# The address distance between the two operands of every fp32r matmul

## The chip, the cores and the metric

The kernel runs on one core of a Trainium2 chip. The metric is the device time of one execution in microseconds (us), of which the median over several executions is given. A profiled execution has, beside its time, a span (from the first to the last instruction) and a trace of every instruction.

A word that is used throughout: a *step* is the time from the start of one matmul to the start of the next one on TensorE.

## The reference, cut to what matters

The kernel computes a two-layer transformer encoder on one sequence of 512 tokens with 1024 channels, in float32. The sizes set the number of matmuls:

```python
def window_gqa_sink(h, w_qkv, w_out, sink):         # layer 0: 16 query heads, 4 key/value heads
    qkv = h @ w_qkv                                 # 1024 -> 1536
    ...
    o, lse = banded_attention(q, k, v, slopes, 1, WINDOW_A, BLOCK_A)
    o = o * jax.nn.sigmoid(lse - sink...)[..., None]
    return o... @ w_out                             # 1024 -> 1024

def dilated_mixture_attention(h, w_qkv, w_out):     # layer 1: three groups of 16 heads
    qkv = (h @ w_qkv).reshape(b, s, N_GROUPS_B, 3, H_B, HEAD_DIM)    # 1024 -> 9216
    ...
    return o... @ w_out

def swiglu(h, w_gate, w_up, w_down):                # after each attention
    return (jax.nn.silu(h @ w_gate) * (h @ w_up)) @ w_down           # 1024 -> 2816 -> 1024

def reference(x, ...):
    for i in range(DEPTH):                          # 2
        x = x + attention_i(rmsnorm(x, norm_mix[i]))
        x = x + swiglu(rmsnorm(x, norm_ffn[i]), w_gate[i], w_up[i], w_down[i])
    return rmsnorm(x, norm_final)
```

## The kernel before

Everything is kept transposed: channels on the 128 partitions, the 512 tokens along the free axis. Each float32 operand is split into a high and a low part of type fp32r (`split`, line 91: ScalarE rounds to the high part, VectorE subtracts to get the low part), and each product is the sum of three fp32r products: high by high, high by low, low by high. This is `mm3` (line 113). It issues its matmuls with 256 moving columns each; with a result of 512 columns that makes six matmuls for one block of 128 by 128 weights.

A matmul has two operands. The *stationary* one (128 columns, 512 bytes in each partition) is put into the array by a weight load; the *moving* one (256 columns, 1024 bytes in each partition) then streams through it. Every matmul of this kernel has a weight load of its own, even where two in a row use the same block.

Three kinds of product go through `mm3`:

- `unit` (line 170), and the output and down projections: the stationary operand is a weight block (`wh` or `wl`), the moving one the activations: `xh`, `xl` (normalised input), `oh`, `ol` (attention output) or `ah`, `al` (the hidden layer of the SwiGLU). In the rows of the profile these are `mm<-xh,wh`, `tp<-xh,wh`, `sc<-ah,wh` and so on: result, moving operand, stationary operand.
- `values` (line 189): here the activations are stationary and the weights move: `psv<-wh,xh`.
- The attention scores in fp32r do not use `mm3` but have the same form: `score_pair` (line 137) in layer 0, with queries `qt` stationary and keys `kt`, `kl` moving, in pieces of 256 or 384 columns; and `scores_a` (line 620) for the first head group of layer 1, with `qs` stationary and `ks`, `kl` moving.

The order of the work on TensorE is written out by hand: generators yield after each block of weights, and `weave` and `spread` place a given number of such pieces between the attention's steps. The SwiGLUs (`swiglu`, line 494) have no such weaving; they are two runs of over 3,000 `mm3` matmuls with nothing between.

Memory is handed out by pools, in the order in which tiles are first asked for, each size rounded up to 32 bytes. Pools stand behind each other: `const` (`x`, `xh`, `xl` and small tables), `wpool` (three buffers of 4096 bytes each for raw weights, `wh` and `wl`), `spool` (small temporaries), and then one pool for the stage that runs: `l0`, `ffn` or `l1`. All operands of the fp32r products are tiles of 2048 bytes in a partition or multiples of it, and they are read in pieces that begin at multiples of 512 bytes from the tile's start. So the distance between the two operands of such a matmul, taken modulo 512, is the same for all matmuls on the same pair of tiles, whichever buffer and whichever block it is. The addresses that the build gives are, as bytes modulo 512:

| tiles | before | with the change |
|---|---|---|
| `wh`, `wl` | 0 | 0 |
| `xh`, `xl` | 192 | 256 |
| `ah`, `al`, `oh`, `ol` | 192 | 256 |
| layer 0: `kt`, `kl` / `qt` | 192 / 192 | 256 / 0 |
| layer 1: `ks`, `kl` / `qs` | 192 / 192 | 0 / 256 |

From this follows the distance, moving minus stationary, modulo 512:

| products | before | with the change |
|---|---|---|
| weights stationary (`unit`, projections), 9,888 matmuls | 192 | 256 |
| activations stationary (`values`), 1,248 matmuls | 320 | 256 |
| fp32r scores, 256 matmuls | 0 | 256 |

Of the kernel before, what the change touches and what calls it, by code (L numbers as in the profile page):

```python
# [9 lines left out]
F32 = mybir.dt.float32  # L10
# [8 lines left out]
H = 16  # L19
# [45 lines left out]
def trunk(ctx, tc, xT, gains, sink, tabs, qsc, wunits, wv, outT):  # L65
# [4 lines left out]
    const = ctx.enter_context(tc.tile_pool(name="const", bufs=1))  # L70
    wpool = ctx.enter_context(tc.tile_pool(name="wpool", bufs=3))
    spool = ctx.enter_context(tc.tile_pool(name="spool", bufs=2))
    psum = ctx.enter_context(tc.tile_pool(name="psum", bufs=2, space=bass.MemoryType.PSUM))
    BUFS = {"mm": 3, "sc": 2, "tp": 2, "ov": 1}

# [2 lines left out]

    x = const.tile([128, NK, S], F32, name="x")
    qs_sb = const.tile([128, 16], F32, name="qs_sb")  # L80
    xh = const.tile([128, NK, S], F32R, name="xh")
    xl = const.tile([128, NK, S], F32R, name="xl")
    g_sb = const.tile([128, 5, NK], F32, name="g_sb")
    sink_sb = const.tile([128, H], F32, name="sink_sb")
    nsink = const.tile([128, H], F32, name="nsink")
    tab = const.tile([128, 1024], F32, name="tab")
    ident = const.tile([128, 128], F32, name="ident")
# [37 lines left out]
    def split_queries(q, pair):  # L125
        for a, (own, other) in enumerate((HALVES, HALVES[::-1])):
            nc.scalar.activation(pair[a][own], q[own], AF.Copy)
            nc.vector.tensor_tensor(pair[a][other], q[own], pair[a][own].bitcast(F32), op=OP.subtract)  # L128

    def split_keys(k, pair, low):  # L130
        for a, (own, other) in enumerate((HALVES, HALVES[::-1])):
            nc.scalar.activation(pair[a][own], k[own], AF.Copy)
            nc.scalar.activation(pair[a][other], pair[a][own].bitcast(F32), AF.Copy)
            nc.vector.tensor_tensor(low[a][own], k[own], pair[a][own].bitcast(F32), op=OP.subtract)
            nc.scalar.activation(low[a][other], low[a][own].bitcast(F32), AF.Copy)
# [34 lines left out]
    def unit(u, hi, lo, tag, done, cuts=(0, NK)):  # L170


        def gen():
            tiles = weight_tiles()
            wh, wl = chunks(tiles, (NK, 128))
            ps = bank(tag)
            for j in range(NK):
                if j in cuts:
                    load(tiles, wunits[u], slice(128 * j, 128 * cuts[cuts.index(j) + 1]))
                mm3(ps, wh[:, j], wl[:, j], hi[:, j, :], lo[:, j, :], j == 0, j == NK - 1)  # L180
                if j == NK - 1:
                    if norm["wait"] is None:
                        done(ps)
                    else:
                        norm["wait"].append(lambda: done(ps))
                yield
        return NK, gen()
# [110 lines left out]
    with tc.tile_pool(name="l0", bufs=2) as pool:  # L298
# [14 lines left out]
        def q_unit(P, i, **kw):  # L313
            def done(ps):
                t = spool.tile([128, S], F32, name="tmp")
                col = 4 * P + i
                nc.vector.scalar_tensor_tensor(t, ps, qs_sb[:, col:col + 1], norm["rb"], op0=OP.mult, op1=OP.mult)
                qk["q", P, i] = [pool.tile([128, S], F32R, name=f"qt{a}", bufs=8) for a in range(2)]
                split_queries(t, qk["q", P, i])
            return unit(5 * P + 1 + i, xh, xl, "mm", done, **kw)  # L320
# [239 lines left out]
    with tc.tile_pool(name="l1", bufs=2) as pool:  # L560
# [9 lines left out]
        def qk_units(p, g):  # L570

            def views(out, *src):
                if g:
                    return (out, *src)
                return (out.rearrange(IN_ORDER, m=16), *[t.rearrange(BY_CLASS, m=16) for t in src])

            def q_done(ps):
                name = "q1" if g else "qa"
                qk["q", p, g] = q = pool.tile([128, S], F32, name=name, bufs=2 if g else 1)
                out, src, rb = views(q, ps, norm["rb"])  # L580

                for to, at in ((slice(4, 32), slice(0, 28)), (slice(0, 4), slice(28, 32))) if g == 0 else [(slice(None),) * 2]:
                    nc.vector.scalar_tensor_tensor(out[..., to], src[..., at], qs_sb[:, 8 + p:9 + p], rb[..., at],
                                                   op0=OP.mult, op1=OP.mult)
                if g == 0:
                    qk["qs", p] = [pool.tile([128, S], F32R, name=f"qs{a}", bufs=1) for a in range(2)]
                    split_queries(q, qk["qs", p])

            def k_done(ps):
                name = "k1" if g else "ka"  # L590
                qk["k", p, g] = k = pool.tile([128, S], F32, name=name, bufs=2 if g else 1)
                out, src, rb = views(k, ps, norm["rb"])
                nc.vector.tensor_tensor(out, src, rb, op=OP.mult)
                if g == 0:
                    qk["ks", p] = [pool.tile([128, S], F32R, name=f"ks{a}", bufs=1) for a in range(2)]
                    qk["kl", p] = [pool.tile([128, S], F32R, name=f"kl{a}", bufs=1) for a in range(2)]
                    split_keys(k, qk["ks", p], qk["kl", p])

            at = u1 + 6 * p + 2 * g
            return [unit(at, xh, xl, "mm", q_done), unit(at + 1, xh, xl, "mm", k_done)]  # L600

        def v_unit(pg, g):
# [356 lines left out]
```

## Time and profile before

| | |
|---|---|
| median of three executions | 1472.33 us (1470.74 to 1473.45) |
| the profiled execution | 1473.99 us |
| its span | 1472.3 us |
| granted TensorE clock, mean | 0.996 |
| TensorE busy | 1453.9 us (99%), 12,820 matmuls |
| VectorE / ScalarE / GpSimd busy | 732.6 / 613.9 / 109.1 us |
| DMA | 128.29 MB, 87 GB/s |
| the two SwiGLUs, from their first matmul on | about 193 to 553 us and 1104 to 1457 us of the span |

The profiled execution is 1.66 us above the median. TensorE is busy all through, so what matters is the step and not the waits. A matmul's own duration in the trace (276 to 287 ns in the large groups) is more than two steps long, because matmuls are pipelined; the rate must be read from the starts or from the length of a piece of the chain of waits divided by its count.

### The profile page before, as it was taken

How to read it: one execution, taken by the hardware profiler on the slowest of the kernel's cores; microseconds unless marked ns; L12 is line 12 of the kernel's file. 1: busy time of each engine (PE TensorE's matmuls, PEld its weight loads, DVE VectorE, ACT ScalarE, POOL GpSimd, SP SyncE). 2: the span in 40 equal slices, each digit the busy share in tenths (PEclk: the TensorE clock that was granted, in tenths of full speed). 3: DMA queues.
4: the chain of work that ended last, by engine and by line, in shares of the span. 5: the costliest groups of instructions: out<-in, count | busy, mean ns of one | idle time of the engine just before them, and what ended most of it. 6: DMA issues, size and time to landing. Idle time of an engine off the chain costs nothing.

```text
span 1472.3 us, 29609 instructions
## 1 busy us (share of the span) xinstructions
PE 1453.9 (99%) x12820; PEld 1426.7 (97%) x12820; DVE 732.6 (50%) x1400; ACT 613.9 (42%) x1126; POOL 109.1 (7%) x152
## 2 busy tenths in 40 slices
PE   8999999999999999999999999999999999999997
PEld 8988999999999999999999999999999999999997
DVE  6776544444443345346556556556464444443223
ACT  6776433322323335445545536536343322332221
POOL 3334200000000010000000000000030000000111
PEclk9999999999999999999999999999999999999998
DMA  6110232323223232312212122222132322232331
GB/s 201 58 59 15 87 101 87 101 101 100 94 87 104 94 111 69 101 63 86 79 67 87 58 87 73 72 87 73 44 116 86 101 101 98 90 101 91 96 103 57
DMA packets 38450, 128.29 MB, mean 87 GB/s; under 512 B 4528, under 2 KB 6832, under 8 KB 38320
## 3 DMA queue, kind: packets, MB, share of 16 engines
q1 hardware_dynamic: 36832, 125.08, 25.5%
q8 instruction: 100, 1.64, 0.4%
q10 hardware_dynamic: 1488, 1.33, 0.3%
q14 instruction: 30, 0.25, 0.1%
HBM read 124.29 MB, written 2.10 MB: 86 GB/s over the span
## 4 chain that ended last, share of the span: by engine, by line
PE 94%; DVE 2%; ACT 2%; issue 1%; DMA 0%; POOL 0%; SPq 0%; DVEq 0%; ACTq 0%; POOLq 0%
PE mm L118 51%; PE sc L118 16%; PE psv L118 10%; PE tp L118 8%; PE sc L696 1%; PE sc L637 1%; PE ov L378 1%; PE ov L751 1%; PE sc L140 1%; PE tp L364 1%; PE tp L659 1%; PE ov L678 1%; ACT pr L353 0%; DVE qt L128 0%; PE tp L738 0%
## 5 line engine op out<-in xcount | busy, mean ns | idle before, releaser
L92 ACT ACTIVATE wh<-wraw 128x1024 fp32r<-128x1024 f32 (+3 forms) x239 | 247.6, 1037 | 599.6 <-PE mm L118 252.0
L93 DVE TENSOR_TENSOR wl<-wraw,wh 128x1024 fp32r<-128x1024 f32 (+3 forms) x239 | 290.2, 1215 | 203.3 <-ACT wh L92 202.7
L118 PE MATMUL mm<-xh,wh 128*128 128x256 f32 x1632 | 331.4, 284 | 0.4 <-ACT xh L217 0.4
L118 PE MATMUL mm<-xh,wl 128*128 128x256 f32 x1632 | 321.6, 279 | 2.6 <-DVE wl L93 2.6
L118 PE MATMUL mm<-xl,wh 128*128 128x256 f32 x1632 | 321.7, 279 | 0.7 <-DVE xl L218 0.6
L118 PEld LDWEIGHTS mm<-xh,wh 128*128 128x128 f32 x1632 | 248.5, 189 | 6.3 <-issue 4.8
L118 PEld LDWEIGHTS mm<-xh,wl 128*128 128x128 f32 x1632 | 247.9, 189 | 3.2 <-DVE wl L93 3.2
L118 PEld LDWEIGHTS mm<-xl,wh 128*128 128x128 f32 x1632 | 248.5, 189 | 1.4 <-DVE xl L218 1.3
L232 POOL TENSOR_TENSOR ssum<-ssum,tmp 128x512 f32<-128x512 f32 x34 | 53.7, 1581 | 994.4 <-ACT tmp L228 979.9
L118 PE MATMUL psv<-wh,xh 128*128 128x256 f32 x288 | 82.8, 287 | 0.0
L118 PE MATMUL psv<-wl,xh 128*128 128x256 f32 x288 | 80.4, 279 | 0.0
L118 PE MATMUL psv<-wh,xl 128*128 128x256 f32 x288 | 80.3, 279 | 0.0
L118 PE MATMUL mm<-ah,wh 128*128 128x256 f32 x374 | 74.9, 277 | 0.0
L118 PE MATMUL mm<-al,wh 128*128 128x256 f32 x374 | 74.7, 276 | 0.0
L118 PE MATMUL mm<-ah,wl 128*128 128x256 f32 x374 | 74.7, 276 | 0.0
L118 PE MATMUL tp<-xh,wh 128*128 128x256 f32 x352 | 68.8, 277 | 0.0
L118 PE MATMUL sc<-xh,wh 128*128 128x256 f32 x352 | 68.7, 277 | 0.0
L118 PE MATMUL tp<-xh,wl 128*128 128x256 f32 x352 | 68.6, 276 | 0.0
L118 PE MATMUL tp<-xl,wh 128*128 128x256 f32 x352 | 68.6, 276 | 0.0
L118 PE MATMUL sc<-xh,wl 128*128 128x256 f32 x352 | 68.5, 276 | 0.0
L118 PE MATMUL sc<-xl,wh 128*128 128x256 f32 x352 | 68.5, 276 | 0.0
L118 PE MATMUL sc<-ah,wh 128*128 128x256 f32 x330 | 66.0, 276 | 0.0
(175 smaller groups left out, 2728.6 us busy)
## 6 DMA issues: line engine op xcount, KB each, us to landing
wraw<-wunits SPq DMA_DIRECT2D x192, 512.0 KB, 3.2
wraw<-wv SPq DMA_DIRECT2D x26, 512.0 KB, 3.3
wraw<-wunits SPq DMA_DIRECT2D x16, 384.0 KB, 3.0
x<-xT SPq DMA_DIRECT2D x8, 256.0 KB, 5.1
wraw<-wunits SPq DMA_DIRECT2D x3, 256.0 KB, 5.5
outT<-x ACTq DMA_DIRECT2D x2, 384.0 KB, 2.7
tab<-tabs SPq DMA_DIRECT2D x1, 512.0 KB, 5.5
outT<-x ACTq DMA_DIRECT2D x2, 256.0 KB, 2.2
```

The costliest lines, as they stand in the source:

```text
L92: nc.scalar.activation(out_h, src, AF.Copy)
L93: nc.vector.tensor_tensor(out_l, src, out_h.bitcast(F32), op=OP.subtract)
L118: nc.tensor.matmul(out[:, cols], a, b[:, cols], start=first and k == 0 and c == 0, stop=last and k == 2, skip_group_check=True)
L140: nc.tensor.matmul(outs[a], qp[a][:, qc], k[a][:, kc], start=first and k is kp, stop=k is low, skip_group_check=True)
L232: nc.gpsimd.tensor_tensor(norm["sum"], norm["sum"], sq, op=OP.add)
L364: nc.tensor.transpose(tp[:, 256 * hf + 128 * i:256 * hf + 128 * i + 128], st["pr"][:, 2 * i + hf, 128 * kb:128 * kb + 128], ident)
L378: nc.tensor.matmul(ov[64 * hf:64 * hf + 64, :256], v0[:, k0 // 128 + kb, vs], st["pt", kb][:, 256 * hf:256 * hf + 256], start=(kb == 0), s ...
L637: nc.tensor.matmul(out, qk["qs", p][a][:, 128 * t:128 * t + 128], kp[k], start=t == ts[0] and k == 0, stop=k == 1, skip_group_check=True)
L659: nc.tensor.transpose(tp[:, (nb * a + kb) * 128:(nb * a + kb) * 128 + 128], st["pr", p, ts][:, a, o + 128 * kb:o + 128 * kb + 128], ident)
L678: nc.tensor.matmul(ov[rows, 128 * t - 64:128 * t + 64], v[:, t - 1 + kb, vs], pt[:, 256 * a + 128 * kb:256 * a + 128 * kb + 128], start=Fa ...
L696: nc.tensor.matmul(ps[a][:, o:o + 128], qk["q", p, 1 + g][rows, cols], qk["k", p, 1 + g][rows, cols], start=(o == 0), stop=True, skip_grou ...
L751: nc.tensor.matmul(ov[rows, 128 * c:128 * c + 128], vals[p // 2, 1 + g][:, c, hv + 64 * a:hv + 64 * a + 64], pts[g][:, 256 * a + 128 * (c ...
```

## The change

No instruction is added, removed or moved: on all five engines the order of the instructions, their operands' shapes and their waits are the same as before. What changes is where tiles lie:

- `sink_sb`, a tile of 64 bytes, is asked for before `xh` and `xl` in place of after `g_sb`. `xh` and `xl` move up by 64 bytes; the sum of the sizes of the `const` pool stays, so `wpool` stays where it was.
- A tile of 64 bytes that nobody uses, `align`, is put at the head of `spool`. Everything from there on (`spool` and the stage pools) moves up by 64 bytes.
- A tile of 256 bytes that nobody uses, `align0`, is put between the keys and the queries of `l0`, and another, `align1`, between the queries and the keys of `l1`.

```diff
     spool = ctx.enter_context(tc.tile_pool(name="spool", bufs=2))
+
+    spool.tile([128, 16], F32, name="align", bufs=1)
...
     qs_sb = const.tile([128, 16], F32, name="qs_sb")
+    sink_sb = const.tile([128, H], F32, name="sink_sb")
     xh = const.tile([128, NK, S], F32R, name="xh")
     xl = const.tile([128, NK, S], F32R, name="xl")
     g_sb = const.tile([128, 5, NK], F32, name="g_sb")
-    sink_sb = const.tile([128, H], F32, name="sink_sb")
...
                 nc.vector.scalar_tensor_tensor(t, ps, qs_sb[:, col:col + 1], norm["rb"], op0=OP.mult, op1=OP.mult)
+                if col == 0:
+                    pool.tile([128, 64], F32, name="align0", bufs=1)
                 qk["q", P, i] = [pool.tile([128, S], F32R, name=f"qt{a}", bufs=8) for a in range(2)]
...
                 name = "k1" if g else "ka"
+                if g == p == 0:
+                    pool.tile([128, 64], F32, name="align1", bufs=1)
                 qk["k", p, g] = k = pool.tile([128, S], F32, name=name, bufs=2 if g else 1)
```

The tiles of the plain float32 products (scores and values of the other head groups, transposes) move too, by 64 or 320 bytes; among them no distance was set on purpose.

## The prediction

> **What bounds the kernel now.** I read the busy times first, then the chain of waits, then the pieces of that chain in order of time, and last the starts of single matmuls.
>
> ```profile
> PE 1453.9 (99%) x12820; PEld 1426.7 (97%) x12820; DVE 732.6 (50%) x1400; ACT 613.9 (42%) x1126; POOL 109.1 (7%) x152
> PE 94%; DVE 2%; ACT 2%; issue 1%; DMA 0%; POOL 0%; SPq 0%; DVEq 0%; ACTq 0%; POOLq 0%
> ```
>
> TensorE is busy for 99% of the span and makes up 94% of the chain. Nothing that it waits for is worth much; only the step itself, from one matmul's start to the next one's, can move the time. So the question is whether the step depends on where the operands lie. A busy figure of 99% doesn't say that each matmul runs at its best, and the pieces of the chain (start, length, what, count) show that it doesn't:
>
> ```profile
> 153.58 39.06 PE mm L118 x330
> ...
> 204.88 10.88 PE mm L118 x96
> ...
> 565.68 42.64 PE psv L118 x360
> ...
> 1071.35 32.47 PE mm L118 x284
> ```
>
> All four are fp32r matmuls with 256 moving columns. In the SwiGLU 10.88 / 96 = 113.3 ns each. The output projection of layer 0 takes 39.06 / 330 = 118.4, the values of layer 1 take 42.64 / 360 = 118.4, and the output projection of layer 1, the same instructions as that of layer 0, takes 32.47 / 284 = 114.3. Between single starts, without the longer first step of a run, these are two rhythms: 113.33 ns, and 117.78 ns on average (three steps that repeat, 353.3 ns together). The next piece of the same view shows them with a third one, and shows that they are states rather than properties of an instruction:
>
> ```profile
> 611.06 0.95 PE sc L637 x8
> 612.02 4.95 PE mm L118 x42
> 616.97 0.96 PE sc L637 x8
> ...
> 631.43 0.44 PE tp L659 x4
> 631.87 2.07 PE mm L118 x18
> 633.93 3.40 PE psv L118 x30
> ```
>
> The scores at line 637, whose operands lie at distance 0, take 0.96 / 8 = 120 ns. The `mm` after them, distance 192, take 4.95 / 42 = 117.9. At 633.93 the values, distance 320, take 3.40 / 30 = 113.3, where at 565.68 the same kind took 118.4. What differs is what went before: the `mm` ahead of 633.93 had come into the fast rhythm, and the values went on in it. A run that starts slow stays slow (330 in a row above), and one that starts fast stays fast for 3,000.
>
> Why would addresses come in? The weight load of the next matmul reads its 512 bytes while the current matmul streams its 1024:
>
> ```profile
> 565.88 0.28 PE L118 MATMUL psv<-wl,oh 128*128 128x256 f32 x1
> 565.89 0.19 PEld L118 LDWEIGHTS psv<-wh,ol 128*128 128x128 f32 x1
> 566.00 0.28 PE L118 MATMUL psv<-wh,ol 128*128 128x256 f32 x1
> 566.00 0.19 PEld L118 LDWEIGHTS psv<-wh,oh 128*128 128x128 f32 x1
> ```
>
> [...]
>
> **The change part by part.** It adds no instruction; DMA, VectorE, ScalarE and GpSimd do the same work. I sort all 11,392 steps in which an fp32r matmul is followed by an fp32r weight load: 7,583 lie at 112 to 115 ns, 3,255 at 116 to 119, 220 at 120 to 126 (143 of them at exactly 120), 64 belong to moving pieces of 384 columns, and 270 are first steps of a run or waits. The stages, as counts of matmuls of line 118:
>
> ```profile
> 29.00:154.00 125.00, 77.75 (x540) 68.59 (x539) 1.00 0.13 44
> 154.00:193.00 39.00, 38.65 (x329) 38.44 (x327) 1.00 0.33 109
> 565.00:608.00 43.00, 42.88 (x364) 42.70 (x364) 1.00 0.27 87
> 608.00:1065.00 457.00, 386.43 (x3081) 366.89 (x3080) 1.00 0.22 75
> ```
>
> What the slower steps cost above 113.33 ns each: layer 0's attention up to 154 us 2.4 us (496 steps), its output projection 1.5 (326), layer 1's attention 11.7 (2,551), the first `up` of the second SwiGLU 0.2 (48), the end 0.2 (46). The sum is 16.1 us. The two long SwiGLU runs hold none of it; they hold 6,140 of the fast steps.
>
> *The scores* leave distance 0 for 256. 143 steps of 120 ns fall to 113.3 at best: 143 x 6.7 = 1.0 us, which is in the 16.1; at worst they stay.
>
> *Weights and values* leave 192 and 320 for 256. No row shows an fp32r matmul at 256, so I bound it by the rows at the three distances that there are. Upper end: the step of distance 0, 120 ns, for all. Middle: the two rhythms stay as they are. Lower end: below 113.3 there is one nearest row, the transposes of 128 columns with 128-column weight loads, 0.44 / 4 = 110 ns from start to start: a step that a load sets with half as long a stream beside it.
>
> The order of the distances decides my choice. The slow step is 120 at 0, 117.8 at 192 and 117.8 at 320; 192 and 320 lie equally far from 0 on a ring of 512, and 256 is the farthest point. In the fast rhythm the step is 113.3 at 192 and at 320 alike, so that looks like a step without collision. I take it that at 256 the collision is gone or so weak that runs settle in the fast rhythm: all steps at 113.3. That is 16.1 us. About 150 of the slow steps lie before 38 us, where TensorE afterwards waits for the splits of the first keys and queries on ScalarE and VectorE anyway, so 0.7 us brings nothing. I round the gain to 15 us: 1459 for the profiled execution (1473.99), which stands 1.7 above the median, hence **1457 us**, and 1454 to 1465 as this case's own range (a third of the slow steps left: 1473.99 - 10 - 1.7 = 1462, and some more for waits that open).
>
> What is late next? With 113.3 ns a weight tile of 48 matmuls is used up in 5.44 us instead of 5.65. It takes ScalarE and VectorE about a microsecond each to split (mean 1037 and 1215 ns), and both are near half busy, so this stays hidden:
>
> ```profile
> L92 ACT ACTIVATE wh<-wraw 128x1024 fp32r<-128x1024 f32 (+3 forms) x239 | 247.6, 1037 | 599.6 <-PE mm L118 252.0
> L93 DVE TENSOR_TENSOR wl<-wraw,wh 128x1024 fp32r<-128x1024 f32 (+3 forms) x239 | 290.2, 1215 | 203.3 <-ACT wh L92 202.7
> ```
>
> **The rivals.**
>
> *The address plays no part (same).* The three rhythms would then be a matter of how a run begins, and the scores would be slow for another reason, as they alternate their buffers. For it: the fast step is the same at two distances, and the values changed nothing when they took over at 633.93. Against it: 120 ns turns up in a row only at distance 0. All steps stay: 1472, give or take 3. [...]
>
> *256 is as bad as 0 (slower).* If the memory repeats its banks every 256 bytes or less, 256 is the same place as 0. It decides everywhere at once: 7,583 x 6.7 + 3,255 x 2.2 = 50.8 + 7.2 = 58 us, 1530 us. For it: 192 and 320 are both 64 off a multiple of 128, so their likeness fits a period of 128 too. Against it: no row of this trace; only that nothing points to 128 or 256 rather than 512.
>
> *The fast rhythm is lost (slower).* After transposes, runs with distance 192 came into the fast rhythm more often than not, while runs of values at 320 never did on their own (42.64 / 360 above); they only kept it. If 256 is like 320 in this, the SwiGLUs start slow and, with nothing to interrupt them, stay slow: 6,140 x 4.45 = 27 us, 1499; with the 1,443 other fast steps 33.7, 1506. One SwiGLU alone: 1486.
>
> *A step below 113.3 (faster still).* If part of the fast step is collision as well, at 110 ns it would be 16.1 + 11,058 x 3.3 = 52 us less: 1420. For it: the transposes. Against it: a step that is the same at 192 and 320, and so probably has no collision left in it. [...]
>
> **How the numbers follow.** Chances: all or most steps at 113.3 0.42; a step below 113.3 0.08; same 0.18; the fast rhythm lost 0.18; 256 as bad as 0 0.14. About 0.2%, 3 us, is what a measurement of this kernel can tell from no change. Faster is 0.42 + 0.08 = 0.50, same 0.18, slower 0.32. The range for 8 in 10 goes from 1450 to 1507: it holds the likeliest case, no change, and the lost rhythm to its full price (0.78), and leaves out 1420 and 1530.
>
> **What would show it.** Right: the output projection of layer 0 (330 matmuls) at about 37.5 us in place of 39.06, the values of layer 1 (360) at about 40.9 in place of 42.64, eight scores of line 637 at 0.91 in place of 0.96, and the SwiGLU's 96 still at 10.88; a mean matmul duration of 276 ns in the groups that show 279 to 287 now. If 10.88 becomes 11.3, the fast rhythm is lost; if 11.5, 256 is as bad as 0; if it falls below 10.8, the fast step still had collisions in it. If none of these lengths moves, the address plays no part.

## The result, and the profile after

The changed kernel takes 1527.07 us (median of five runs, 1526.7 to 1527.35) against 1472.18 us for the kernel before: a ratio of 1.0373, with a 95% interval of 1.0358 to 1.0389. It is slower by 55 us, where 1457 was forecast and 1450 to 1507 given as the range. The profiled execution took 1527.35 us, its span 1525.6. From here on *distance* is that from the stationary to the moving operand in bytes, and unless a number above 255 is given, modulo 256; why modulo 256 is the subject of what follows.

The busy times and the chain's shares of the changed kernel:

```profile
PE 1509.6 (99%) x12820; PEld 1483.5 (97%) x12820; DVE 732.2 (48%) x1400; ACT 612.2 (40%) x1126; POOL 110.2 (7%) x152
PE 97%; DVE 1%; ACT 1%; DMA 0%; issue 0%; DVEq 0%; SPq 0%; ACTq 0%
```

VectorE, ScalarE and GpSimd are busy as before, within 2 us. All of the loss is on TensorE, which is busy 55.7 us longer with the same 12,820 matmuls. The pieces of the chain of waits of the changed kernel (start, length, what, count; line 118 has become 120, line 637 has become 643), the same places as those shown of before:

```profile
154.84 39.79 PE mm L120 x330
...
207.44 11.52 PE mm L120 x96
...
587.08 43.43 PE psv L120 x360
...
633.39 0.96 PE sc L643 x8
634.35 5.04 PE mm L120 x42
...
1102.49 34.34 PE mm L120 x284
```

Length divided by count is 120.6, 120.0, 120.6, 120.0, 120.0 and 120.9 ns. Before, these were 118.4, 113.3, 118.4, 120, 117.9 and 114.3. There is one step left, 120 ns, everywhere: in the SwiGLU, in the projections, in the values and in the scores, which had it before. Of the 11,392 steps sorted in the prediction, 7,583 lay at 112 to 115 ns, now 23 do; at 116 to 119 were 3,255, now 614 (nearly all among the first ten steps of a run); at 120 to 126 were 220, now 10,425. The runs that start below 120 reach it within about ten steps and stay.

The account, worked out from the starts of all fp32r matmuls in the profiled executions: what the steps up to 126 ns cost above 113.33 ns each, by kind of product; what the longer ones (first steps of a run, waits; some 270) cost above 113.33; and what is left of the span (with the 64 pieces of 384 columns, whose steps stay alike).

| kernel | weights stationary | values | scores | longer steps | span | rest of the span |
|---|---|---|---|---|---|---|
| before | 10.0 | 5.2 | 1.0 | 32.8 | 1472.3 | 1423.3 |
| after | 63.6 | 7.9 | 1.1 | 30.4 | 1525.6 | 1422.6 |

The rest is the same within 0.7 us: the span grows by 53.3, the steps by 56.4, and the longer ones shrink by 2.4. Not all of these 2.4 us are waits. The trace of before has a time of half clock at 555.6 us, in which 15 steps take 213 ns (together 1.5 us above 113.33 each). Two of the kernels below have one there too: the 48 matmuls that it falls into take 7.17 us before, 7.20 in "the pads alone" (from 562.98 on) and 7.20 in "the distance back" (from 555.23 on), but 5.76 in the changed kernel and 5.61 to 5.74 in "xh and xl alone", "128", "64" and "112 for the weights". The changed kernel has a half clock at 10.2 us instead, which costs little: its longer steps among the first 200 matmuls cost 7.3 us, those of before 6.7. TensorE's waits for the low part of the weights fell from 3.4 to 1.8 us. The two windows, of before and of the changed kernel (window, busy time and count of PE and PEld, then DVE, ACT, POOL, granted clock, DMA):

```profile
555.60:559.00 3.40, 3.40 (x18) 3.40 (x18) 3.40 (x6) 1.86 (x3) 0.00 (x0) 0.50 0.00 0
```

```profile
10.20:17.00 6.80, 6.17 (x29) 5.88 (x28) 6.80 (x6) 6.34 (x12) 6.13 (x6) 0.50 0.69 242
```

### The profile page after: what moved, and what is told of

The parts are those of the page before. It is cut to its first block, busy times and chain, and to the rows that moved or that the text cites. A ratio compares the mean times of both kernels' runs of the same rounds, so it can differ in the third digit from the quotient of the medians.

```text
span 1525.6 us, 29609 instructions
## 1 busy us (share of the span) xinstructions
PE 1509.6 (99%) x12820; PEld 1483.5 (97%) x12820; DVE 732.2 (48%) x1400; ACT 612.2 (40%) x1126; POOL 110.2 (7%) x152
## 4 chain that ended last, share of the span: by engine, by line
PE 97%; DVE 1%; ACT 1%; DMA 0%; issue 0%; DVEq 0%; SPq 0%; ACTq 0%
PE mm L120 53%; PE sc L120 16%; PE psv L120 9%; PE tp L120 8%; PE ov L382 1%; PE sc L142 1%; PE tp L368 1%; PE sc L702 1%; PE sc L643 1%; PE ov L757 1%; PE tp L665 1%; PE ov L684 1%; PE tp L744 0%; PE ssq L238 0%; DVE x L478 0%; DMA x<-xT 0%
## 5 line engine op out<-in xcount | busy, mean ns | idle before, releaser
L120 PE MATMUL mm<-xh,wh 128*128 128x256 f32 x1632 | 339.0, 289 | 1.0 <-ACT xh L219 1.0
L120 PE MATMUL mm<-xh,wl 128*128 128x256 f32 x1632 | 330.0, 284 | 1.1 <-DVE wl L95 1.1
L120 PE MATMUL mm<-xl,wh 128*128 128x256 f32 x1632 | 330.0, 284 | 0.3 <-DVE xl L220 0.3
L120 PEld LDWEIGHTS mm<-xh,wh 128*128 128x128 f32 x1632 | 255.1, 192 | 6.9 <-issue 4.8
L120 PEld LDWEIGHTS mm<-xh,wl 128*128 128x128 f32 x1632 | 255.4, 193 | 1.6 <-DVE wl L95 1.6
L120 PEld LDWEIGHTS mm<-xl,wh 128*128 128x128 f32 x1632 | 255.2, 192 | 0.5 <-DVE xl L220 0.5
```

Of the source, the lines that this page charges most:

```text
L120: nc.tensor.matmul(out[:, cols], a, b[:, cols], start=first and k == 0 and c == 0, stop=last and k == 2, skip_group_check=True)
```

## The experiments

The theory after the result: the step depends on the distance, with a period of 256 bytes or less, so that 256 is the same as 0. Its rivals: the absolute place of the activations decides (they moved to multiples of 256); the change does harm by something else than the distance; and, within the theory, a period of 128 or 64.

### Every distance, without the transformer

```diff
+    def product(at, dist, n):
+        for r in range(n):
+            j = r // 2 % 4
+            s0 = at // 4 + 128 * j
+            m0 = (at + dist) // 4 + 512 * j + 256 * (r % 2)
+            c = 256 * (r % 2)
+            nc.tensor.matmul(ps[:, c:c + 256], sta[:, s0:s0 + 128], mov[:, m0:m0 + 256], ...)
+    for at, dist in CASES:      # 0 to 496 by 16; then base 64, then finer distances
+        turns(4); product(at, dist, 48); sums(4); product(at, dist, 48); turns(3); sums(1); product(at, dist, 48)
```

> Leaves out the whole computation; it only runs fp32r matmuls (128 stationary columns, 256 moving ones, a weight load each) in stretches of 48 at one distance, at distances 0 to 496 in steps of 16 bytes with the stationary operand at 0 modulo 512, then six distances with the stationary operand at 64, then a few distances that are no multiple of 16. Each distance is run three times, after three different beginnings. Period 128 (only the distance modulo 128 counts): 120 ns at 0, 128, 256 and 384, and 113.3 to 118 elsewhere. Period 256: 120 ns at 0 and 256 alone, and 128 and 384, the farthest points, at least as fast as 64 and 192. Period 512 with a second bad point at 256 for some other reason: 120 at 0 and 256, no likeness between 64 and 320. The moving operand's own place and not the distance: with the stationary operand at 64, distance 192 (moving at 256) is at 120 and distance 256 (moving at 320) is not. By distance, 256 is at 120 there too.

The three beginnings of each distance are four transposes, four one-column sums, and three transposes with a sum. The chain of this run shows each stretch of 48 matmuls as a piece; about 0.1 us of each belongs to its longer first step. The second stretch (behind the sums) at distances 0, 64, 112, 128 and 192, then at 256, 320, 368 and 448; the first of the two lines that begin at 241.84 and 248.08 is the first stretch at 192:

```profile
21.53 5.86 PE mm L100 x48
...
97.01 5.76 PE mm L100 x48
...
153.89 5.57 PE mm L100 x48
...
172.39 5.86 PE mm L100 x48
...
241.84 5.46 PE mm L100 x48
...
248.08 5.76 PE mm L100 x48
...
323.77 5.86 PE mm L100 x48
...
399.07 5.76 PE mm L100 x48
...
455.96 5.57 PE mm L100 x48
...
550.15 5.76 PE mm L100 x48
```

The lengths at 0 and 256, 64 and 320, 112 and 368, 192 and 448 are the same pair by pair. The mean of the last 24 steps of each stretch, in ns; one number where the three beginnings agree within 0.4:

| distance | step | distance | step |
|---|---|---|---|
| 0 | 120 | 128 | 118.6 / 120 / 118.5 |
| 16 | 116.7 / 116.7 / 118.8 | 144 | 118.6 |
| 32 | 116.7 | 160 | 118.8 / 117.2 / 117.5 |
| 48 | 118.3 | 176 | 119.2 |
| 64 | 117.8 | 192 | 113.3 / 117.8 / 117.8 |
| 80 | 118.3 / 120 / 120 | 208 | 119.2 |
| 96 | 120 | 224 | 118.3 |
| 112 | 113.3 | 240 | 117.1 |

From 256 to 496 the column repeats, in all but two of 48 stretches (one at 272, one at 288) within 0.4 ns. With both operands moved by 64 bytes, the steps at 0, 64, 128, 192, 256 and 320 are those of their distances (120, 117.8, 118.6, 117.8 or 113.3, 120, 117.8). So the period is 256 bytes, not 64 or 128 and not 512, and for shifts of both operands by 64 bytes the distance decides and not the place; smaller shifts were not tried. Under a period of 256 the far points 128 and 384 were expected to be at least as fast as 64 and 192; at 118.6 to 120 ns they are not. Two things are new: 112 is the one distance in this list at which all beginnings end in the fast step, and at 192 a stretch goes either to 113.3 or to 117.8 within its first five steps and stays there. That is the fast and the slow rhythm of the kernel before. Which of the two it will be does not follow from the kind of beginning alone: behind four transposes a stretch at 192 ended at 113.3 here, and at 117.8 with both operands moved by 64 bytes.

### Finer distances, unequal distances, other widths

(The edit is shown against the first scan.)

```diff
-CASES = [(0, d) for d in range(0, 512, 16)] ...
+CASES = [(fixed(d), 256) for d in range(0, 256, 4)] \
+    + [(own_and_next(o, n), 256) for o, n in ((0, 112), (112, 0), (0, 192), (192, 0), (192, 112), (112, 192))] \
+    + [(fixed(d), w) for w in (128, 384) for d in (0, 64, 112, 192)]
```

> Leaves out the whole computation, as the first scan does. Distances 0 to 252 in steps of 4 bytes, two beginnings each; then six cases in which the distance of a matmul to its own stationary operand differs from that to the stationary operand of the next matmul, which is loaded while it streams; then moving pieces of 128 and of 384 columns at 0, 64, 112 and 192. Collision of the stream with the load of the next operand: own 0 and next 112 gives 113.3 ns, own 112 and next 0 gives 120, own 0 and next 192 gives 113.3 or 117.8, own 192 and next 0 gives 120, and of 192 and 112 the second number decides. Something within one matmul (its own operands): the other way round. [...] A distance below 113.3 ns would show that the fast rhythm had collisions left.

The multiples of 16 came out as in the first scan, but for the first stretch of all (it has steps of 213 ns in it) and three distances: at 64 one of the two beginnings now ended at 113.3, at 192 both ended at 117.8, and at 32 one did. No distance but 112 was fast in both beginnings; away from multiples of 16 all lie between 117.5 and 123.5. No stretch of 256 columns went below 113.3. With 384 moving columns the distance hardly counts any more: 173.3 ns at 0, 64 and 112, and 174.7 and 176.7 at 192. The first stretch of 128 columns, at distance 0, ended at 111.7 ns; the others fell into a time of half clock (granted clock 0.50, steps of 213 ns) of some 82 us, and say nothing of the distance; the run's mean clock, 0.961 over 1075.3 us, comes to 84 us at half clock.

The third question was which distance sets the step, that to the own or that to the next stationary operand. For a matmul whose own stationary operand lies at one distance and whose successor's lies at another, the second stretches were (own 0 and next 112, then own 112 and next 0, then own 192 and next 112):

```profile
843.67 5.81 PE mm L111 x48
...
856.35 5.76 PE mm L111 x48
...
894.26 5.68 PE mm L111 x48
```

That is 118.8, 117.5 and 115.4 ns a step: neither the own nor the next distance alone gives the step (by either it would be 113.3 in one of the first two rows). With 0 and 192, where every operand begins at a multiple of 64 bytes, it was 118.3 (own 0, next 192) and 117.5. So the answers that were expected, 113.3 in one order and 120 in the other, both failed, and what sets the step there stays open.

### Half of the change: xh and xl alone

```diff
+    sink_sb = const.tile([128, H], F32, name="sink_sb")
     xh = const.tile([128, NK, S], F32R, name="xh")
     xl = const.tile([128, NK, S], F32R, name="xl")
     g_sb = const.tile([128, 5, NK], F32, name="g_sb")
-    sink_sb = const.tile([128, H], F32, name="sink_sb")
```

> Only xh and xl go to distance 256; ah, al, oh, ol stay at 192 and the scores at 0. Distance at work: the 4,224 gate and up matmuls go from 113.3 to 120 ns (28 us), the other 3,648 with xh or xl, about a third of them fast before, cost 13 us: about 1513. The SwiGLU's down projection stays at 113.3. If the float32 tiles or the scratch tiles that moved were the cause: about 1472.

1509.66 us, ratio 1.0256 (1.022 to 1.0292). The chain inside the first SwiGLU, `up` and `gate` (moving `xh`, `xl`, now at 256) first, then the down projection (moving `ah`, `al`, still at 192):

```profile
206.40 11.52 PE mm L118 x96
...
502.42 14.96 PE mm L118 x132
```

120.0 and 113.3 ns; 1513 us in all was expected. Each product pays for its own distance: the steps of the products with `ah`, `al`, `oh` and `ol` as moving operands cost 0.3 us more than before, those with `xh` and `xl` 36.6.

### The other half: the pads alone

```diff
+    spool.tile([128, 16], F32, name="align", bufs=1)
...
+                if col == 0:
+                    pool.tile([128, 64], F32, name="align0", bufs=1)
...
+                if g == p == 0:
+                    pool.tile([128, 64], F32, name="align1", bufs=1)
```

> The other half of the change: the pads without the move of xh and xl. The products with xh and xl stay at 192 (values at 320), those with ah, al, oh and ol go to 256, as do the scores. If every matmul pays for its own distance and nothing else, the halves add up: the move of xh and xl alone cost 37.4 us of the 54.9, which leaves 17.5, so 1490 us; the down projections and output projections at 120 ns and gate and up at 113.3. If the slow step spreads from run to run (or both halves are needed for it), gate and up become slow too, and the time is above 1500 us.

1487.8 us, ratio 1.0098 (1.0081 to 1.0114); 1490 was expected. The same two places, with the roles exchanged:

```profile
205.74 10.88 PE mm L120 x96
...
507.96 15.84 PE sc L120 x132
```

113.3 and 120.0 ns. By the two ratios the halves cost 37.7 and 14.4 us, together 52 of the 55. Most of what is missing lies in products that this run leaves at 192, the weight products with `xh` and `xl`: their steps cost 5.2 us above 113.33 each here and 8.0 before.

### The distance back, the place kept

(The edit is shown against the changed kernel.)

```diff
+    gap = ctx.enter_context(tc.tile_pool(name="gap", bufs=1))
+    gap.tile([128, 16], F32, name="align")
     wpool = ctx.enter_context(tc.tile_pool(name="wpool", bufs=3))
     spool = ctx.enter_context(tc.tile_pool(name="spool", bufs=2))
-
-    spool.tile([128, 16], F32, name="align", bufs=1)
```

> The changed kernel with one move: the weights (raw, high and low) also lie 64 bytes further, so that the activations stay exactly where the change has put them while the distance of weight products and values is back at 192 and 320. If the distance between the operands decides, the time is that of the kernel before, 1472 us, with the SwiGLU's matmuls at 113.3 ns. If the absolute place of the activations decides (they lie at multiples of 256 here as in the changed kernel), it stays at 1527 us.

1472.47 us, ratio 0.9996 (0.9987 to 1.0005). The place in the chain that took 11.52 us with the change:

```profile
204.97 10.88 PE mm L121 x96
```

All activations lie where the change has put them, and the loss is gone. The place of the weights alone is not the cause either, as the change had left them where they were before. This settles it: the loss comes from the distance between weights and activations, 256 in place of 192, and from nothing else that the change moves.

### 128

```diff
+    small = ctx.enter_context(tc.tile_pool(name="small", bufs=2))
...
+    spool.tile([128, 32], F32, name="align", bufs=1)
...
+    sink_sb = const.tile([128, H], F32, name="sink_sb")
+    nsink = const.tile([128, H], F32, name="nsink")
     xh = const.tile([128, NK, S], F32R, name="xh")
```

> All products with weights at distance 128 (values 384); the scores stay at 0; three small tiles of the norm stand ahead of the weight pool for that. Period 128: every step 120, 1526 to 1530. Period 256 or 512: 128 is no bad place, 1457 to 1475.

1514.61 us, ratio 1.0289 (1.0253 to 1.0326). The place in the SwiGLU:

```profile
206.72 11.39 PE mm L120 x96
```

118.6 ns, as at 128 in the scan (118.6 or 120). On a ring of 256 bytes 128 is the farthest point from 0, and it is slow. So the idea behind the forecast, that the far point is the good one, is wrong with the right period too.

### 64: weights and values exchange their distances

```diff
+    small = ctx.enter_context(tc.tile_pool(name="small", bufs=2))
...
+    spool.tile([128, 16], F32, name="align", bufs=1)
...
+    sink_sb = const.tile([128, H], F32, name="sink_sb")
     xh = const.tile([128, NK, S], F32R, name="xh")
```

(The three small tiles of the norm come from `small`, which lies ahead of `wpool`, in place of `spool`.)

> The same at distance 64 (values 448). Period 128: 64 is the same place as 192, so 113.3 and 117.8 in some mixture, 1457 to 1506, nearest to 1472. Period 256: 64 is like the 320 of the values before, which came into the fast rhythm on their own in no run: up to 1506.

1499.28 us, ratio 1.0185 (1.015 to 1.0221). The SwiGLU, and the 360 values of layer 1:

```profile
205.95 11.31 PE mm L120 x96
...
578.77 41.05 PE psv L120 x360
```

The SwiGLU falls into the slow rhythm and stays there, 117.8 ns; the values, now at 448, come into the fast one, 114.0 with their first steps, where they took 118.4. So the two rhythms belong to the distances 64 and 192, not to the kinds of product: at 192 both long runs of the SwiGLUs are in the fast rhythm after three steps, at 64 neither comes into it in over 3,000. The kernel before has its weights on the good one of the two, and its values pay for it with the other, since their distance is the negative of the weights'.

### 112 for the weights

```diff
+    def both(pool, name, n, at=4):
+        t = pool.tile([128, 2 * n * S + 8], F32R, name=name, bufs=1)
+        return [t[:, k:k + n * S].rearrange("p (k s) -> p k s", k=n) for k in (at, at + n * S)]
...
-    xh = const.tile([128, NK, S], F32R, name="xh")
-    xl = const.tile([128, NK, S], F32R, name="xl")
+    xh, xl = both(const, "xh", NK)
...                                         # oh, ol and ah, al likewise, and a pad in spool
```

> Distance 112 modulo 256 for all products with stationary weights, which makes the values 144; the scores stay at 0. High and low parts share one tile each, shifted by 16 bytes. If the first scan carries over, all 9,888 matmuls with stationary weights run at 113.3 ns whatever came before them, the 1,248 values at 118.6, the 256 scores at 120: of the 16.1 us of slow steps about 10 go, the values lose 1: 1462 to 1464, about 0.6% faster than before. If the rhythm in the kernel is ruled by how runs begin and not by the distance: 1472 to 1506.

1472.21 us, ratio 0.9997 (0.9987 to 1.0006): no change, where a gain of some 9 us was expected. The output projection of layer 0 now settles in the fast step (322 of its 330 steps), and the SwiGLU is as before, but the values, at 144, lost what the others gained:

```profile
204.05 10.88 PE mm L123 x96
...
563.31 43.43 PE psv L123 x360
```

43.43 / 360 = 120.6 ns, in a cycle of six steps. By the account above: weights stationary 10.0 to 7.1 us, values 5.2 to 7.9. At 112 the first steps of a run, mostly 7 to 14 of them at 114 to 123 ns, also remain, and most runs of the attention have only 6 to 48.

### 112 for all

```diff
-    def weight_tiles():
-        return (wpool.tile([128, 1024], F32, name="wraw"), wpool.tile([128, 1024], F32R, name="wh"),
-                wpool.tile([128, 1024], F32R, name="wl"))
+    def weight_tiles(at=8):
+        i = at + 1024 * (next(turn) % 3)
+        return (wpool.tile([128, 1024], F32, name="wraw"), ring[:, i:i + 1024], ring[:, 3072 + i:4096 + i])
...
-            w = [load_unit(wv[2 * i + k], (4, 256)) for k in range(2)]
+            w = [load_unit(wv[2 * i + k], (4, 256), 0) for k in range(2)]
```

> As the kernel with 112 for stationary weights, but the high and low weight parts of the values are written 32 bytes lower in their buffers (one tile holds all three buffers of each part), so that the values too lie at 112 modulo 256 in place of 144; scores stay at 0. If the distance decides, the six-step cycle of the values (114, 119, 122, 126 ns, mean 120) goes and their runs settle at 113.3 after the first 9 to 12 steps: 1,248 steps by about 5 ns, 6 us, so 1466 us and the first kernel that is faster than before. If the values' slowness belongs to their form (activations stationary) and not to the distance, the time stays at 1472 us.

1498.19 us, ratio 1.0178 (1.0158 to 1.0198): 1.8% longer, and for a reason that neither theory named. The waits of TensorE for split weights in this kernel, and those in the kernel before (us in total, times, longest):

```profile
PE psv L125 <- DVE wh L98: 7.5, 9, 1.0
PE psv L125 <- ACT wh L97: 7.4, 4, 2.7
PE mm L125 <- DVE wh L98: 4.8, 8, 0.9
...
PE mm L125 <- ACT wh L97: 0.4, 2, 0.2
```

```profile
PE mm L118 <- DVE wl L93: 3.4, 4, 1.2
```

TensorE waits 20.1 us for split weights in place of 3.4. After one of the longest waits, 2.7 us, the clock was halved for 3.4 us (columns as in the windows above):

```profile
959.90:962.60 2.70, 0.07 (x1) 0.07 (x1) 1.91 (x6) 2.70 (x10) 0.00 (x0) 1.00 0.00 0
964.00:967.40 3.40, 3.40 (x17) 3.40 (x17) 2.68 (x4) 3.33 (x7) 0.00 (x0) 0.50 0.53 158
```

The likely reason of the waits, argued from the layout and not tried: a buffer of the values, 32 bytes lower, overlaps the end of the buffer below it, so it can be filled only when that one too has been used. The steps answer the question by themselves, as the waits are in another column: weights stationary 7.0, values 6.1 (118.6 ns on average), scores 0.9 us, longer steps 55.6 (32.8 before). The values went from 119.9 ns at 144 to 118.6 at 112, not to 113.3; whole runs of them settle at 116.7, at 120, or in cycles like 121, 117, 120, 115. So the expectation fails in its second half too: in this kernel the values at 112 are not fast, though the weights are.

### Why are the values slow at 112?

```diff
+            if order == "values":
+                (ah, al), (bh, bl) = hi_lo(sta, 0, 512, r % 4), hi_lo(mov, dist // 4, 256, r)
+                tok = slice(128 * (r // 4), 128 * (r // 4) + 128)
+                for k, (a, b) in enumerate(((ah, bh), (ah, bl), (al, bh))):
+                    nc.tensor.matmul(ps[:, :256], a[:, tok], b, ...)
```

> Not the transformer (its computation is left out): stretches of 48 fp32r matmuls with 256 columns on two pairs of tiles, at distances 0 to 240 in steps of 16, each distance behind transposes and behind one-column sums, first in the order and with the operands' places of the values (stationary high, high, low against moving high, low, high, another token block after every four), then in those of the unit. No other engine writes in between. Theory (the order of the operands counts beside the distance): in the order of the values the step is about 118 ns at 112 and 120 at 144, as in the two kernels with 112, and 113.3 to 115 at 192, where the unit's order has 113.3 at 112. Rival (the distance alone counts, and something else in the kernel slows the values): both orders give 113.3 at 112, 117.8 or 113.3 at 64 and 192, and 118 to 120 at 144.

The second stretch at 112 in the order of the values, the one at 128 behind it, and the second at 112 in the order of the unit:

```profile
114.87 5.57 PE mm L105 x48
...
127.35 5.87 PE mm L105 x48
...
317.49 5.57 PE mm L111 x48
```

Both orders give 113.3 ns at 112, and at the other distances they agree stretch by stretch within 0.2 ns, but for the first stretch of all, in which only 16 matmuls lie between 16.7 and 20.2 us. The order of the operands is not the reason.

```diff
-    sta = const.tile([128, 2 * 2048], F32R, name="sta")
     mov = const.tile([128, 2 * 2048 + 64], F32R, name="mov")
+    sta = const.tile([128, 2 * 2048], F32R, name="sta")
...
+        nc.scalar.activation(sta[:, :128], x[:, 0, :128], AF.Copy)
```

> The stretches of the run with two orders again, with two changes: the tile of the moving operands lies below that of the stationary ones (as weights lie below the activations in the values of the kernel), and each distance has a third beginning, in which the first matmul waits idle until ScalarE has rewritten its stationary operand. If it matters which operand lies lower, distance 112 is slow in all three beginnings here (about 118 to 120 ns) and another distance (144, its mirror image) may be fast. If the beginning decides, 112 gives 113.3 behind transposes and sums, as before, and 117 to 120 behind the idle time. If neither, all three give 113.3 and the slow values at 112 stay unexplained.

Behind transposes and behind sums 112 gives 113.3 ns with the moving tile below as well, in both orders; 144 gives 118.5 to 118.8. Which operand lies lower is not the reason. The third beginning had no idle time in it and tells nothing of a beginning from standstill. The next run has that idle time:

```diff
-        nc.scalar.activation(sta[:, :128], x[:, 0, :128], AF.Copy)
+        nc.scalar.activation(sta, flat, AF.Copy)
```

> The run with the moving tile below, whose third beginning had no idle time in it (ScalarE had rewritten the first block long before it was needed), with that mended: ScalarE rewrites the whole stationary tile, which needs all matmuls before it to be over, so TensorE stands idle for some 4 us and begins again from standstill, as a run of values in the kernel does. If the beginning decides, the step at 112 settles at 117 to 120 ns behind the idle time and at 113.3 behind transposes and sums. If it does not, 113.3 in all three, and why the values of the kernel with everything at 112 are slow stays open.

Windows of this run, at distance 112: the stretch behind the sums, the idle time, the first 3.4 us after it and the rest of the stretch (columns as in the windows above):

```profile
193.00:198.50 5.50, 5.50 (x50) 5.50 (x50) 0.00 (x0) 0.00 (x0) 0.00 (x0) 1.00 0.00 0
198.50:202.50 4.00, 0.32 (x3) 0.12 (x2) 0.00 (x0) 3.59 (x1) 0.00 (x0) 1.00 0.00 0
202.60:206.00 3.40, 3.40 (x17) 3.40 (x18) 0.00 (x0) 0.00 (x0) 0.00 (x0) 0.57 0.00 0
206.00:209.50 3.50, 3.50 (x30) 3.50 (x30) 0.00 (x0) 0.00 (x0) 0.00 (x0) 0.93 0.02 5
```

After this standstill of 3.75 us the granted clock was 0.57 in the first 3.4 us and 0.93 in the next 3.5, which comes to 3.4 us at half clock; 17 matmuls lie in the first window and 30 in the second. Then the stretch at 112 settled at 113 and 114 ns. A beginning from standstill is not the reason either. Why the values stay slow at 112 inside the kernel is left open: the order of the operands, which one lies lower, and the standstill are excluded in these stretches, in which hardly anything works beside TensorE. What other engines do at the same time was not tested, but the SwiGLU reaches 113.3 ns at 112 while ScalarE and VectorE split its weights.

The addresses of the builds show another difference, which no run tried. In all these stretches the stationary operand begins at a multiple of 256 bytes. In "112, all" that of the values begins 16 bytes past one, in the kernel with 112 for the weights 144 bytes past one. In each of the other kernels it begins at a multiple of 64, and there the values take a step that the scan has at their distance (117.8 at 64, 120 at 0, 118.6 at 128, 113.3 or 117.8 at 192). Only the two whose stationary operand of the values lies 16 bytes off a multiple of 32 depart from the scan: 120 in place of 118.6 at 144, 118.6 in place of 113.3 at 112. So the place may count beside the distance, in steps finer than the 64 bytes by which the scan moved it; a scan with the stationary operand at 16 would tell.

No version came out ahead of the kernel before. By the account, weights at 112 (7.1 us as in the run with 112) with values at 192 (1.9 us in the run with 64) would leave 9.9 us above the fast step with the scores' 0.9, against 16.2 now, some 6 us less. That is an estimate from two different kernels; it needs separate places for the values' weights with room between the buffers, and was not tried.

All kernels in one account (us, columns as above):

| kernel | distance of weights / values | weights stationary | values | scores | longer steps | span | rest |
|---|---|---|---|---|---|---|---|
| before | 192 / 64 | 10.0 | 5.2 | 1.0 | 32.8 | 1472.3 | 1423.3 |
| after | 0 / 0 | 63.6 | 7.9 | 1.1 | 30.4 | 1525.6 | 1422.6 |
| xh, xl alone | 0 and 192 / 0 and 64 | 46.7 | 7.1 | 0.7 | 30.5 | 1507.9 | 1422.9 |
| pads alone | 192 and 0 / 64 and 0 | 23.9 | 6.0 | 0.8 | 32.9 | 1486.8 | 1423.2 |
| distance back | 192 / 64 | 8.6 | 5.2 | 1.0 | 33.1 | 1470.8 | 1422.9 |
| 128 | 128 / 128 | 52.0 | 6.4 | 1.1 | 30.8 | 1512.7 | 1422.4 |
| 64 | 64 / 192 | 40.3 | 1.9 | 1.0 | 31.6 | 1497.6 | 1422.8 |
| 112, weights | 112 / 144 | 7.1 | 7.9 | 0.9 | 31.5 | 1470.7 | 1423.3 |
| 112, all | 112 / 112 | 7.0 | 6.1 | 0.9 | 55.6 | 1495.2 | 1425.6 |

But for the last row, the rest is the same within a microsecond: nearly every difference between these kernels is in the steps and, for "112, all", in the waits and in the time of half clock.

## Why the prediction was wrong

*What bounds the kernel.* Right. TensorE's step sets the time: the span grew by 53.3 us and the steps by 56.4, and the rest of the span did not change.

*"Why would addresses come in?"* The four lines shown for it have a load and a matmul at the same time: the load that begins at 565.89 lasts 0.19 us, to 566.08, and the matmul that uses it is recorded from 566.00 on. That the two collide was the author's supposition; no line and no run shows a collision. The runs show that the step depends on the distance (113.3 ns at 112, 120 at 0), and with the unequal distances (118.8 and 117.5 ns for 0 and 112) that neither the own nor the next load alone sets it; they do not show the mechanism.

*Two rhythms, kept once reached, and the third step of 120 ns at distance 0.* Right, and now shown outside the kernel: 113.3 or 117.8 at 192, settled in the first five steps of a stretch, and 120 at 0.

*"192 and 320 lie equally far from 0 on a ring of 512, and 256 is the farthest point."* This is the step that failed. The ring is 256 long: 256 gives 120 ns in all of its stretches, like 0. The trace of before held the three distances 0, 192 and 320 and could not tell a ring of 512 from one of 256; the prediction said so under its rival and then gave the ring of 512 three times the chance, for no row. Its second half failed by itself: even on the right ring the farthest point, 128, is slow (118.6), while 112 is fast and 96 is at 120. The step is no smooth function of the distance, so no order of three distances could give a fourth.

*The gain of 16.1 us, of which 15 would remain.* There was no gain to collect. At distance 112 all stretches outside the kernel reach 113.3, yet the kernel with its weights there kept 7.1 of the 10.0 us, in the first steps of each run. The prediction treated all slow steps as a rhythm that another distance removes. At 112 the slow rhythm is gone, but there the way into the fast step is itself 7 to 14 steps long in most runs, and short runs end before or soon after it.

*The rival "256 is as bad as 0".* It happened, priced at 58 us and 1530. It cost 56.4 us in the steps: 614 first steps stay at 116 to 119, which the price had counted at 120. The longer steps gave back 2.4 us that the price left out, of which 1.5 us are the half clock at 555.6 us of before, which is no effect of the distance as far as the traces show. The chance of 0.14 was too small, as no row spoke for a period of 512 rather than 256. That the memory repeats its banks was a supposition: the runs show the period of the step (120 ns at 0 and at 256), not where it comes from.

*The rival "the address plays no part".* Excluded: the "distance back" run gives 1472.47 where only 64 bytes of weight address differ from the changed kernel's 1527, and in the first scan the same matmul with the same load takes 113.3 ns at distance 112 and 120 at 0.

*The rival "the fast rhythm is lost".* Not at 256, but real: at 64 the SwiGLU is in the slow rhythm throughout, and the time is 1499.28 us, where the prediction had put 1499 on just that. That the two agree to the microsecond is partly luck: the weight products cost 30.3 us more there, not 27, and the values (3.3) and the longer steps (1.2) cost less.

*The rival "a step below 113.3".* Excluded for 256 columns in all distances tried: the lowest step is 113.3. The 110 ns of its price are measured on transposes of 128 columns; that the load sets that step, and that 256 columns could come down to it, was the author's supposition, and no run shows either.

*The signs to look for.* These were right: 11.5 us for the SwiGLU's 96 was announced as the sign of "256 is as bad as 0", and the piece measures 11.52.

## What to carry to other kernels

In these runs, where fp32r matmuls of 256 columns each come with a weight load of their own, the distance between the two operands' addresses modulo 256 bytes was worth 6% of the step: 113.3 ns at 112 against 120 at 0. With both operands at multiples of 256 the step was 120 ns, and a layout that looks like harmless alignment cost 55 us here. Read the step from the length of chain pieces divided by their count, in each stage, and compare it between stages that run the same instruction form: a busy share of 99% shows nothing of this. Where a step depends on an unknown function of an address, measure all of the distances in one small run before reasoning on from two or three of them.

## What the runs showed of the hardware

- In the two scans the step of an fp32r matmul of 256 columns with its own weight load depended on the distance of the operands with a period of 256 bytes, between 113.3 and 123.5 ns, and not smoothly: 120 at 96, 113.3 at 112, 118.6 or 120 at 128. This was measured with the stationary operand at multiples of 64 bytes.
- At 192 and at 64 the same stretch settled at 113.3 or at 117.8 ns, in the first scan within five steps, and the kind of beginning alone did not tell which; inside the kernel before a run kept its 113.3 ns for 3,000 matmuls.
- With 384 columns the dependence was nearly gone: 173.3 ns at 0, 64 and 112, and 174.7 and 176.7 at 192.
- A stretch in which the own and the next stationary operand lay at different distances (0 and 112) took 118.8 or 117.5 ns by which of them came first, so neither of the two distances alone set the step.
- In the run with idle time a standstill of TensorE of 3.75 us was followed by 3.4 us at half clock; the mean clock of that run, 0.930 over 787.1 us with 32 standstills, comes to as much for each of them (0.07 x 787.1 x 2 / 32 = 3.4). In "112, all" a wait of 2.7 us was followed by 3.4 us at half clock, too. At half clock the steps of before were 213 ns. In the finer scan a half clock lasted some 82 us (mean clock 0.961).
